# Channel cosines and sines folded into the Fourier weights, h folded over positions ahead of the product

## The chip, the cores and the metric

The kernel runs on one core of one Trainium2 chip. The core has a matrix engine (TensorE, PE in the profile, with its weight loads as PEld), a vector engine (VectorE, DVE), a scalar engine (ScalarE, ACT), a general one (GpSimd, POOL) and a queue engine for transfers (SyncE, SP). The metric is the time of one execution on the device in microseconds, as the median of several runs.

## The reference, cut to what matters

Two sequences (a prompt of 256 and a sample of 1024 positions, each with 16 meta positions ahead of it) go through one encoder layer with shared weights. The change is in branch A and in where the gates are made:

```python
h = rms_norm(x, norm_mix_g)
z = h @ w_in                      # q | k | v | fourier channels | attn gate | fourier gate
f = z[..., o2:o3]                 # 512 channels, 4 groups of 128
...
fg = f.astype(jnp.float32).reshape(b, l, N_FOURIER_GROUPS, FOURIER_GROUP)
y = jnp.real(jnp.fft.fftn(fg, axes=(1, 3), norm='ortho'))   # over positions and channels of a group
...
merged = g_attn * a + g_four * fo
```

The real part of the two-dimensional transform is cos(position) cos(channel) minus sin(position) sin(channel). Cosines are even and sines odd in the position, so a sequence of L positions can be folded first: position n plus position L - n for the cosine part, minus for the sine part. That leaves 521 positions of 1040 for the sample and 137 of 272 for the prompt. In the same way 65 cosines and 63 or 64 sines are enough for a group of 128 channels.

## The kernel before, in words

The kernel multiplies in split form. A float32 operand is stored as a high part, rounded to the format fp32r, and a low part, the rest; `three` (L220) adds high x high, high x low and low x high into one bank of PSUM. So each product of 128 input rows costs three matmuls. A "unit" of weights is 128 output columns for all eight blocks k of 128 input rows: 24 matmuls for one range of positions.

**Stage A** (`stage_a`, L307) normalises x, transposes it (`transpose_pair`, L279) and keeps the result h as `hT[c]`, high and low parts, for three chunks c: 512 and 512 positions of the sample, and the prompt's 256 with the 16 meta positions. As soon as a part of h is there, `fgemm` (L359) multiplies it with four units of Fourier weights: chunk 0 in two halves of 256 positions, the prompt's chunk with 272, chunk 1 with 512. The results go to SBUF as `fT` and `fTp`.

**The next stage** runs three generators, each of which yields a cost after every piece of work. `fourier` (L492) folds f over positions on DVE (`fold`, L499), multiplies it with the channels' cosines and sines (`chan`, L522, in plain float32, tile by tile of 128 positions), and then with the tables of the positions (from L590), which come by the POOL queue. `q_pass` (L753) and `kv_pass` (L694) make q, k and v. `weave(main, side, share)` (L142) puts gate work between their pieces: each cost that main yields, times the share, is spent on steps of `gate_gen` (L432). That generator makes the 16 units of gate logits for one set of chunks and stores them in DRAM; a step is three matmuls. In this stage it works on chunk 0. `ahead` starts the next generator's loads at a given yield of the present one (`QSTART`, L48, is that of q).

**Attention** (L794) writes out its own order of instructions for TensorE, ScalarE and VectorE. Between its steps a `Filler` (L155) places gate steps for chunks 1 and 2, as many as the costs in `FILL` (L430) allow. After it come the merge with the gates, the output projection and the feed-forward part, whose instructions the change doesn't touch.

Outside the parts whose order is written out, a planner places each instruction in its engine's queue: the earliest in program order goes first among those that it expects to be ready. So a load or a matmul of later work may stand ahead of earlier work that is expected to wait. Each engine then takes its queue strictly in order.

SBUF is handed out by `Slots` (L66): 27 single slots and 7 triples, each slot 1056 float32 columns wide. A slot that is given back goes to the end of a queue; who gets it next waits until the last reader is done. The high and low parts of h take 8, 8 and 6 slots for the three chunks.

## Time and profile before

| | |
|---|---|
| Median of 3 runs | 1727.22 us (1727.02 to 1728.23) |
| The profiled execution | 1727.39 us, its span 1725.6 us |
| Granted TensorE clock | 0.996 of full |
| Busy: PE, DVE, ACT, POOL | 97%, 65%, 42%, 16% of the span |
| Instructions | 25871, of them 9837 matmuls |
| HBM traffic | 140.68 MB read, 55.42 MB written |

The span runs from the first to the last instruction; the time of the execution holds a little more at both ends. A row of a group names line, engine, operation, what is written from what, the shapes and the count, then busy time and the mean duration of one. Matmuls overlap, so a mean duration is more than the distance between two of them. A float32 matmul that isn't split is recorded as two. Idle time of an engine is put down to the instruction that ended it.

### The profile page before, as it was taken

The page shows a single profiled execution, that of the slowest core. Times are in us where ns is not written, and L with a number is a line of the kernel's source. Part 1 is how long each engine was busy: PE and PEld are TensorE (multiplying, and loading weights), DVE is VectorE, ACT ScalarE, POOL GpSimd, SP SyncE. Part 2 cuts the span into 40 slices and gives each one's busy share as a digit, 9 for nine tenths or more (in the row PEclk, how much of TensorE's full clock was granted, in tenths as well). Part 3 has the DMA queues.
Part 4 walks back from the last instruction along what each step waited for, and adds up shares of the span by engine and source line. Part 5 has one row for each costly group of instructions (what it writes and reads, how often), then busy time and mean ns, then how long its engine had stood idle before and what let it go on. Part 6 is the DMA issues. An engine that isn't in the chain of part 4 may idle for free.

```text
span 1725.6 us, 25871 instructions
## 1 busy us (share of the span) xinstructions
PE 1679.1 (97%) x9837; PEld 1495.5 (87%) x9837; DVE 1116.3 (65%) x2089; ACT 719.4 (42%) x1429; POOL 278.7 (16%) x321
## 2 busy tenths in 40 slices
PE   7999999999999999989989999999999999999997
PEld 6888879878888888878879999999999998888886
DVE  5423544568888885652479676667666768765685
ACT  6322333456666665451355222222222234444444
POOL 3001333210130212663353000000000000000002
PEclk9999999999999999999999999999999999999999
DMA  5144331312112235534442222322232237653534
GB/s 191 57 140 145 116 116 51 124 53 71 50 57 63 65 116 195 177 110 135 160 158 82 84 71 91 103 91 83 95 103 80 76 123 259 204 179 99 161 99 153
DMA packets 90509, 197.80 MB, mean 115 GB/s; under 512 B 9773, under 2 KB 40137, under 8 KB 90384
## 3 DMA queue, kind: packets, MB, share of 16 engines
q1 hardware_dynamic: 81168, 178.97, 31.5%
q10 hardware_dynamic: 7824, 12.53, 2.1%
q0 software_dynamic: 1392, 4.63, 0.9%
q8 instruction: 77, 1.26, 0.3%
q14 instruction: 48, 0.39, 0.1%
HBM read 140.68 MB, written 55.42 MB: 114 GB/s over the span
## 4 chain that ended last, share of the span: by engine, by line
PE 83%; DVE 7%; issue 3%; ACT 3%; POOL 3%; DMA 2%; SPq 0%; POOLq 0%; ACTq 0%; DVEq 0%
PE i L225 10%; PE i L226 10%; PE i L227 10%; PE o L227 5%; PE o L226 5%; PE o L225 5%; PE g L225 4%; PE S L892 4%; PE g L227 4%; PE g L226 4%; PE pt L826 3%; PE pv L846 2%; PE pv L847 2%; PE wo L226 2%; PE wo L227 2%
## 5 line engine op out<-in xcount | busy, mean ns | idle before, releaser
L1345 ACT CAST w<-wi 128x512 fp32r<-128x512 f32 x168 | 103.9, 621 | 272.0 <-PE i L227 221.1
L225 PE MATMUL i<-A,w 128*128 128x384 f32 x616 | 208.9, 339 | 3.0 <-ACT w L1345 2.7
L227 PE MATMUL i<-A,w 128*128 128x384 f32 x616 | 208.0, 338 | 2.3 <-POOL w L1347 2.3
L226 PE MATMUL i<-A,w 128*128 128x384 f32 x616 | 208.2, 338 | 0.0
L227 PE MATMUL i<-Ah,w 128*128 128x256 f32 x616 | 173.0, 281 | 0.0
L226 PE MATMUL i<-Al,w 128*128 128x256 f32 x616 | 173.0, 281 | 0.0
L225 PE MATMUL i<-Ah,w 128*128 128x256 f32 x616 | 172.7, 280 | 0.0
L828 ACT CAST pT<-pt 128x512 fp32r<-128x512 f32 x156 | 90.7, 582 | 96.4 <-PE pt L826 91.4
L829 DVE TENSOR_TENSOR pT<-pt,pT 128x512 fp32r<-128x512 f32 x156 | 106.9, 686 | 27.1 <-ACT pT L828 25.0
L1347 DVE TENSOR_TENSOR w<-wi,w 128x512 fp32r<-128x512 f32 x154 | 105.2, 685 | 29.0 <-ACT w L1345 28.6
L234 POOL TENSOR_SCALAR fin0r<-fin0ss 128x1 f32<-128x1 f32 x1 | 0.8, 788 | 754.0 <-ACT X L242 754.0
L225 PEld LDWEIGHTS i<-A,w 128*128 128x128 f32 x616 | 116.5, 189 | 3.6 <-ACT w L1345 2.9
L897 DVE TENSOR_REDUCE sm<-S 128x1 f32<-128x1040 f32 (+1 forms) x80 | 86.5, 1081 | 51.1 <-PE S L892 46.8
L227 PEld LDWEIGHTS i<-A,w 128*128 128x128 f32 x616 | 116.2, 189 | 3.2 <-POOL w L1347 3.2
L226 PEld LDWEIGHTS i<-A,w 128*128 128x128 f32 x616 | 116.5, 189 | 0.0
L225 PEld LDWEIGHTS i<-Ah,w 128*128 128x128 f32 x616 | 116.0, 188 | 0.4 <-ACT w L1345 0.4
L227 PEld LDWEIGHTS i<-Ah,w 128*128 128x128 f32 x616 | 116.1, 189 | 0.0
L226 PEld LDWEIGHTS i<-Al,w 128*128 128x128 f32 x616 | 116.0, 188 | 0.0
L904 ACT ACTIVATE p<-S,sm 128x1040 f32<-128x1040 f32 (+1 forms) x80 | 80.2, 1002 | 33.6 <-DVE sm L897 29.2
L826 PE MATMUL pt<-ident,p 128*128 128x128 f32 (+1 forms) x624 | 93.4, 272 | 0.0
L227 PE MATMUL o<-wfo,act 128*128 128x512 f32 (+1 forms) x212 | 82.0, 387 | 2.3 <-DVE act L1479 2.3
L826 PEld LDWEIGHTS pt<-ident,p 128*128 128x128 f32 (+1 forms) x624 | 72.4, 134 | 10.7 <-DVE pT L829 0.2
(762 smaller groups left out, 4444.9 us busy)
## 6 DMA issues: line engine op xcount, KB each, us to landing
wi<-w_fi SPq DMA_DIRECT2D x48, 512.0 KB, 3.4
wg<-w_g SPq DMA_DIRECT2D x32, 512.0 KB, 3.7
act_d<-sc SPq DMA_DIRECT2D x77, 192.0 KB, 1.9
act<-act_d SPq DMA_DIRECT2D x37, 320.0 KB, 3.3
wfo<-w_fo SPq DMA_DIRECT2D x21, 512.0 KB, 5.2
X<-act_d SPq DMA_DIRECT2D x31, 320.0 KB, 3.0
act_d<-sc SPq DMA_DIRECT2D x77, 128.0 KB, 1.7
gate<-gs ACTq DMA_DIRECT2D x32, 256.0 KB, 2.0
```

Source lines behind the costliest of these rows:

```text
L225: mm(out, sh, mh, start=first and i == 0, stop=False)
L226: mm(out, sh, ml, start=False, stop=False)
L227: mm(out, slo, mh, start=False, stop=last and i == n - 1)
L826: nc.tensor.transpose(pt[:rows, h * P : (h + 1) * P], me.ps4[h][:, col : col + rows], self.ident[:])
L828: nc.scalar.copy(pT[:rows, :512], pt[:rows, :])
L829: nc.vector.tensor_tensor(pT[:rows, 512:1024], pt[:rows, :], f32(pT[:rows, :512]), op=ALU.subtract)
L846: nc.tensor.matmul(me.pv[:], vst, pT[:rows, :512], start=j == 0, stop=False)
L892: nc.tensor.matmul(S[:, base + lo : base + hi], hq, self.kT[seq][g][v][:, lo:hi], start=v == 0, stop=v == 1)
L897: nc.vector.tensor_reduce(nb, S[:, base : base + L], axis=AX.X, op=ALU.max, negate=True)
L904: self.last_exp = nc.scalar.activation(p, S[:, base : base + L], AF.Exp, bias=nb, accum_out=total)
L1345: nc.scalar.copy(w[:, :512], src)
L1347: eng.tensor_tensor(w[:, 512:1024], src, f32(w[:, :512]), op=ALU.subtract)
```

## The change

The channels' cosines and sines are multiplied into the Fourier weights on the chip. `channels` does this with 32 float32 matmuls on the transposed weights `w_ft`, and splits the result into high and low parts `wc`: for each k 260 cosine columns (4 groups of 65) and 252 sine columns (4 of 63).

Before the product, h itself is folded over positions. For each k, `folds` copies the meta positions on ACT, adds the high and low parts of h on POOL, makes sum and difference on DVE, and splits both (`eo`) on ACT and DVE. Two folds are issued between the units of the last product of stage A, the others between the products that use them.

`fourier_in` multiplies the folded h with the new weights: six blocks of positions (four of 128, one of 41, one of 128), for each the even part with 260 columns and the odd part with 252, three matmuls each, accumulated over all eight k in six banks of PSUM. The result, evicted in high and low parts, takes the place of what `chan` made. The tables of positions are rearranged to fit, with the weight of the two ends halved, and the rows of the output weights likewise.

In stage A, `first` takes the place of `fgemm`, with the same ranges of positions (256 in place of 272 for the prompt): it makes the first four units of gate logits and stores them. `gate_gen` makes the other twelve. The numbers that pace the gate work (`FILL`, the shares of `weave`, `QSTART`) are changed with it.

```diff
-QSTART = 22
+QSTART = 60
...
+N_FIRST = 4
...
+NS, NP_ = 521, 137
+FN = 544 + NP_
...
-            if len(wf) < 4:
-                wf.append(self.load_split(a["w_f"][len(wf)], D, "wf", nc.vector))
+            if len(wf) < N_FIRST:
+                wf.append(self.load_split(a["w_g"][len(wf)], D, "wf", nc.vector))
...
-        self.fT = [sl.get(f"fT{g}") for g in range(4)]
-        self.fTp = [sl.get(f"fTp{g}") for g in range(2)]
...
-        def fgemm(c, lo, hi):
+        def first(c, lo, hi, then=None):
...
-            for g in range(4):
-                wh, wl = wf[g]
-                pf = ps.tile([P, 512], F32, tag="mm", name=f"f{c}_{g}")
+            for u in range(N_FIRST):
+                wh, wl = wf[u]
+                pf = ps.tile([P, 512], F32, tag="mm", name=f"f{c}_{u}")
...
-                if c < 2:
-                    b = N_META + 512 * c + lo
-                    nc.scalar.copy(self.fT[g][:, b : b + n], pf[:, :n])
...
-                    fp = self.fTp[g // 2]
-                    nc.scalar.copy(fp[:, b + N_META : b + 272], pf[:, :256])
-                    nc.vector.tensor_copy(fp[:, b : b + N_META], pf[:, 256:272])
-                    nc.vector.tensor_copy(self.fT[g][:, :N_META], pf[:, 256:272])
+                st = self.small.tile([P, 512], F32, tag="stage", name=f"fg{u}_{c}")
+                nc.scalar.copy(st[:, :n], pf[:, :n])
+                nc.scalar.dma_start(self.gates[u][c][:, lo:hi], st[:, :n])
+                if then is not None:
+                    sl.put(wh, wl)
+                    if u % 2 == 0:
+                        next(then)
...
-        fgemm(0, 0, 256)
...
-        fgemm(0, 256, 512)
...
-        fgemm(2, 0, 272)
+        self.T = self.const.tile([P, P], F32, name="T")
+        nc.sync.dma_start(self.T[:], a["chan"])
+        wt = [sl.get("wft") for _ in range(4)]
+        for g in range(4):
+            nc.sync.dma_start(wt[g][:, :D], a["w_ft"][g])
+        first(2, 0, 256)
         tiles(4)
-        fgemm(1, 0, 512)
...
-    FILL = {"s": 610, "p": 400, "end": 640, "drain": 900}
+        self.channels(ps, wt)
+        sl.put(*wt)
+        self.fold = self.folds()
+        next(self.fold)
+        first(1, 0, 512, self.fold)
...
+    def channels(self, ps, wt):
...
+        self.wc = [(sl.get("wch", F32R, "s"), sl.get("wcl", F32R, "s")) for _ in range(4)]
+        for k in range(KD):
+            pt = ps.tile([P, 512], F32, tag="mm", name=f"wc{k}")
+            for g in range(4):
+                c = slice(g * P, (g + 1) * P)
+                nc.tensor.matmul(pt[:, c], wt[g][:, k * P : (k + 1) * P], self.T[:], start=True, stop=True)
+            p4 = pt[:].rearrange("p (g c) -> p g c", g=4)
+            for src, b, w in ((p4[:, :, :65], 0, 65), (p4[:, :, 65:], 260, 63)):
+                h, l = (x.v(4, w, k % 2 * 512 + b) for x in self.wc[k // 2])
+                nc.scalar.copy(h, src)
+                nc.vector.tensor_tensor(l, src, f32(h), op=ALU.subtract)
+        self.wz = self.small.tile([P, 512], F32R, tag="stage", name="wz")
+        nc.gpsimd.memset(f32(self.wz[:, 260:]), 0.0)
+        nc.gpsimd.tensor_copy(self.wz[:, :260], f32(self.wc[0][0][:, :260]))
...
+    def folds(self):
...
+        vec, pool = nc.vector.tensor_tensor, nc.gpsimd.tensor_tensor
+        hs = [sl.get("hs", F32, "s") for _ in range(2)]
+        ep, od = sl.get("ep", F32, "s"), sl.get("od", F32, "s")
...
+        for i, (h, l) in enumerate(zip(t["hi"], t["lo"])):
+            per = t["per"]
...
+            pool(out, *src, op=ALU.add)
...
+        for k in range(KD):
+            s, p = hs[k % 2], ep[:, 8 : 8 + LP + 1]
+            m = m32[:, k * N_META : (k + 1) * N_META]
+            for x, L in ((s, LS), (p, LP)):
+                nc.scalar.copy(x[:, :N_META], m)
+                nc.scalar.copy(x[:, L : L + 1], m[:, 0:1])
+            for c, x, lo in ((0, s, N_META), (1, s, N_META + 512), (2, p, N_META)):
+                h, l = (f32(y) for y in self.hpair(self.hT[c], k, 0, CH_N[c]))
+                pool(x[:, lo : lo + CH_N[c]], h, l, op=ALU.add)
+            out = self.eo[k] = []
+            for z, op in ((e, ALU.add), (o, ALU.subtract)):
+                vec(z[:, :NS], s[:, :NS], s[:, LS : NS - 2 : -1], op=op)
+                vec(z[:, 544:FN], ep[:, 8 + NP_ - 1 : 7 : -1], p[:, NP_ - 1 :], op=op)
+                h, l = (sl.get("eo", F32R, "s") for _ in range(2))
+                nc.scalar.copy(h[:, :FN], z)
+                vec(l[:, :FN], z, f32(h[:, :FN]), op=ALU.subtract)
+                out.append((h, l))
+            yield
...
+    def fourier_in(self, ps):
...
+        cols = [(j * P, P) for j in range(4)] + [(512, 41), (553, P)]
+        banks = [ps.tile([P, 512], F32, tag="mm" if j < 4 else "tr", name=f"u{j}") for j in range(6)]
+        for k in range(KD):
+            while k not in self.eo:
+                next(self.fold)
+            parts = self.eo.pop(k)
+            w = [x[:, k % 2 * 512 : k % 2 * 512 + 512] for x in self.wc[k // 2]]
+            for j, (b, m) in enumerate(cols):
+                for odd, (h, l) in enumerate(parts):
+                    s = slice(260, 512) if odd else slice(260)
+                    out, hm, lm = banks[j][:m, s], h[:, b : b + m], l[:, b : b + m]
+                    if k or odd:
+                        nc.tensor.matmul(out, hm, w[0][:, s], start=False, stop=False)
+                    else:
+                        nc.tensor.matmul(banks[j][:m, :], hm, self.wz[:], start=True, stop=False)
+                    nc.tensor.matmul(out, hm, w[1][:, s], start=False, stop=False)
+                    nc.tensor.matmul(out, lm, w[0][:, s], start=False, stop=odd == 1 and k == KD - 1)
+                yield 0
+            for x in parts:
+                sl.put(*x)
+            if k + 2 < KD:
+                next(self.fold)
+            if k % 2:
+                sl.put(*self.wc[k // 2])
+        next(self.fold, None)
+        ue = [sl.get("ue", F32R) for _ in range(3)]
+        uo = [sl.get("uo", F32R) for _ in range(3)]
...
+        for j, (_, m) in enumerate(cols):
...
+            for base, w, src in ((0, 64, ev[:, :, :64]), (256, 1, ev[:, :, 64:65])):
+                hv = u.v(4, w, b + base)[:m]
+                lv = u.v(4, w, b + 260 + base)[:m]
+                nc.scalar.copy(hv, src)
+                nc.vector.tensor_tensor(lv, src, f32(hv), op=ALU.subtract)
+            b = j % 2 * 512
+            u = uo[j // 2]
+            src = banks[j][:m, 260:512]
+            nc.scalar.copy(u[:m, b : b + 252], src)
+            nc.vector.tensor_tensor(u[:m, b + 256 : b + 508], src, f32(u[:m, b : b + 252]), op=ALU.subtract)
+        self.U = ue, uo
+        yield 6000
...
+    FILL = {"s": 455, "p": 350, "end": 480, "drain": 900}
...
-        order = list(range(16))
+        order = list(range(N_FIRST, 16))
...
-        E = [sl.get(f"fe{j}") for j in range(2)]
-        O = [sl.get(f"fo{j}") for j in range(2)]
-        Ep, Op = sl.get("fep"), sl.get("fop")
...
-        def fold(src, b, L, e, eb, o, ob, eng):
...
-            eng.tensor_tensor(
-                e[:, eb + 1 : eb + h], src[:, b + 1 : b + h], src[:, b + L - 1 : b + h : -1], op=ALU.add
-            )
-            eng.tensor_tensor(
-                o[:, ob + 1 : ob + h], src[:, b + 1 : b + h], src[:, b + L - 1 : b + h : -1], op=ALU.subtract
-            )
...
-        for g in range(4):
-            b = (g % 2) * 521
-            fold(self.fT[g], 0, LS, E[g // 2], b, O[g // 2], b, nc.vector)
-            fold(self.fTp[g // 2], (g % 2) * 272, LP, Ep, g * 137, Op, g * 137, nc.vector)
-            yield 1
-        sl.put(*self.fT, *self.fTp)
...
-        def chan(seq):
...
-            for j in range(nt):
...
-                        e, o = Ep[:, b : b + m], Op[:, b : b + m]
-                    nc.tensor.matmul(pe[:m, g * 65 : (g + 1) * 65], e, T[:, :65], start=True, stop=True)
-                    nc.tensor.matmul(po[:m, g * 64 : (g + 1) * 64], o, T[:, 65:129], start=True, stop=True)
...
-                yield 2000
...
-        for j, m in enumerate((P, 9)):
+        for j, m in enumerate((P, 41)):
             nc.gpsimd.dma_start(tp[j][:m, : 4 * NLP], a["pos_p"][j, :m])
-        us = yield from chan("s")
-        up = yield from chan("p")
-        sl.put(*E, *O, Ep, Op)
+        yield from self.fourier_in(ps)
+        us = self.U
...
-        ms = [P, 9]
+        ms = [P, 41]
...
-                    (u_of(kind, p, up, j, m), (tp[j][:m, tb : tb + NLP], tp[j][:m, tb + NLP : tb + 2 * NLP]))
+                    (u_of(kind, p, us, 5 - j, m), (tp[j][:m, tb : tb + NLP], tp[j][:m, tb + NLP : tb + 2 * NLP]))
...
-        sl.put(*tp, *up[0], *up[1])
+        sl.put(*tp)
...
             weave(ahead(self.fourier(ps), QSTART, q_pass), gates, 0.6)
-            weave(ahead(q_pass, KVSTART, kv_pass), gates, 0.62)
-            weave(kv_pass, gates, 0.6)
+            weave(ahead(q_pass, KVSTART, kv_pass), gates, 0.35)
+            weave(kv_pass, gates, 0.7)
...
-    t["chan"] = np.concatenate([np.cos(ang) * r, np.sin(ang[:, :64]) * r], axis=1).astype(np.float32)
...
+    t["chan"] = np.concatenate([np.cos(ang) * r, np.sin(ang[:, 1:64]) * r], axis=1).astype(np.float32)
...
         ang = 2 * np.pi * ((n * ls[None]) % L) / L
-        keep = (n <= L // 2) * (L ** -0.5)
+        keep = ((n >= 0) & (n <= L // 2)) * (L ** -0.5) * np.where(n % (L // 2) == 0, 0.5, 1.0)
...
-    cp, sp = pos(LP, 2, np.arange(1, NLP + 1))
+    i = np.arange(P)
+    n = np.concatenate([127 - i, np.where((i >= 32) & (i <= 40), 168 - i, -1)])
+    cp, sp = pos(LP, n, np.arange(1, NLP + 1))
...
-        "w_f": units(w[:, 768:1280]),
+        "w_ft": w[:, 768:1280].T.reshape(4, P, D),
```

More of the change, by code (lines that the diff above doesn't have):

```diff
@@ L414, in stage_a @@
         nc.sync.dma_start(xm[:N_META, :D], a["meta_tokens"])
-        fgemm(0, 0, 256)
+        first(0, 0, 256)
         tiles(2)
@@ new lines, in folds @@
+    def folds(self):
+        nc, sl = self.nc, self.sl
+        vec, pool = nc.vector.tensor_tensor, nc.gpsimd.tensor_tensor
+        hs = [sl.get("hs", F32, "s") for _ in range(2)]
+        ep, od = sl.get("ep", F32, "s"), sl.get("od", F32, "s")
+        m32 = self.const.tile([P, KD * N_META], F32, name="m32")
+        t = self.hT[2]
+        for i, (h, l) in enumerate(zip(t["hi"], t["lo"])):
+            per = t["per"]
+            n = min(per, KD - per * i)
+            src = [f32(x.v(per, t["n"])[:, :n, 256:272]) for x in (h, l)]
+            out = m32[:, i * per * N_META : (i * per + n) * N_META].rearrange("p (k c) -> p k c", k=n)
+            pool(out, *src, op=ALU.add)
+        e, o = ep[:, 304 : 304 + FN], od[:, :FN]
+        for x in (e, o):
+            nc.gpsimd.memset(x[:, NS : 512 + 32], 0.0)
+        self.eo = {}
+        yield
[16 more added lines that the diff above has]
+                out.append((h, l))
+            yield
+        sl.put(*hs, ep, od)
```

62 lines of the change are left out of this document (16 added, 46 removed).

## The prediction

> **What bounds the kernel now.** I read the page's table of engines first, then the stretches by engine, then what TensorE waited for, and last the order of single instructions around the change.
>
> ```profile
> span 1725.6 us, 25871 instructions
> PE 1679.1 (97%) x9837; PEld 1495.5 (87%) x9837; DVE 1116.3 (65%) x2089; ACT 719.4 (42%) x1429; POOL 278.7 (16%) x321
> ```
>
> ```profile
> 60.00:100.00 40.00, 39.04 (x218) 32.49 (x217) 16.14 (x40) 12.85 (x34) 4.56 (x8) 1.00 0.16 39
> 100.00:150.00 50.00, 50.00 (x302) 40.50 (x302) 14.71 (x29) 12.54 (x25) 3.72 (x7) 1.00 0.62 206
> 150.00:260.00 110.00, 108.68 (x531) 89.11 (x530) 51.13 (x91) 32.81 (x58) 36.92 (x43) 1.00 0.29 104
> 360.00:650.00 290.00, 287.33 (x1729) 241.41 (x1728) 235.78 (x348) 185.36 (x335) 46.98 (x40) 1.00 0.23 69
> ```
>
> A stretch's columns are its length, then the busy time of PE, PEld, DVE, ACT and POOL, the granted clock, and the DMA share and rate. From 60 to 650 us TensorE is busy nearly all the time at clock 1.00; it waits for almost nothing in the stages that the change rewrites:
>
> ```profile
> PE qtr L778 <- DVE qs L769: 1.3, 1, 1.3
> PE g L225 <- ACT fT L373: 1.0, 1, 1.0
> ```
>
> These are all its waits between 60 and 260 us. So the time falls by what is taken off TensorE, as long as the vector engines keep up, and rises by each new wait. VectorE is idle over half of the time up to 260 us, but has 235.8 of 290 us in attention.
>
> **The price of a matmul.** Matmuls overlap, so I take the distance between starts, not a mean duration.
>
> ```profile
> 39.62 0.28 PE L227 MATMUL f<-hT0h,wfl 128*128 128x256 f32 x1
> ...
> 44.34 0.28 PE L225 MATMUL f<-hT0h,wfh 128*128 128x256 f32 x1
> ```
>
> ```profile
> 77.63 0.39 PE L225 MATMUL f<-hT1h,wfh 128*128 128x512 f32 x1
> ...
> 82.97 0.39 PE L227 MATMUL f<-hT1h,wfl 128*128 128x512 f32 x1
> ```
>
> The first pair is 40 steps apart: 4.72/40 = 0.118 us for 256 columns. The second is 23 steps: 5.34/23 = 0.232 us for 512.
>
> **TensorE, part by part.** One unit over one range of positions is 8 k times 3 products = 24 matmuls, so four units are 96.
>
> - Removed, the Fourier product of L359: two ranges of 256 (192 x 0.118 = 22.7 us), one of 272 (96 x 0.125, scaled, = 12.0), one of 512 (96 x 0.232 = 22.3): 57.0 us.
> - Added in its place, four gate units over three ranges of 256 and one of 512: 34.0 + 22.3 = 56.3 us.
> - Removed from the later gate work, the same four units, two ranges of 512 and one of 256: 44.5 + 11.3 = 55.8 us. Of this 22.3 us were woven into the Fourier, q and k/v stages, and 33.6 us are attention's filler.
> - Added, the folded product: 8 k x 6 position blocks x 6 matmuls = 288, of 260 or 252 columns, six of them 512: 282 x 0.118 + 6 x 0.232 = 34.7 us.
>
> ```profile
> 85.14 0.33 PE L538 MATMUL ues<-T,fe 128*128 128x65 f32 x2
> ...
> 86.64 0.39 PE L539 MATMUL uos<-T,fo 128*128 128x64 f32 x2
> 86.84 0.48 PE L225 MATMUL g<-hT0h,wgh 128*128 128x512 f32 x1
> ```
>
> ```profile
> 97.23 0.28 PE L538 MATMUL ues<-T,fe 128*9 128x65 f32 x2
> ...
> 98.03 0.28 PE L539 MATMUL uos<-T,fo 128*9 128x64 f32 x2
> ```
>
> ```profile
> 59.05 1.47 PE L287 MATMUL x4tr<-ident,h 128*128 128x128 f32 x12
> ```
>
> - Removed, the channel product of L522: a tile of eight float32 matmuls takes 86.84 - 85.14 = 1.70 us, five such tiles 8.5 us, and the two tiles of nine rows 0.9 us each: 10.3 us.
> - Added, channels: 32 float32 matmuls of 128 columns, not in this trace. By the channel rows (16 records in 1.70 us, two per matmul) they take 6.8 us; were the time in proportion to columns, 13.6. The transposes have 128 columns and the same 0.11 us a record (1.47 us for 12), so I take 7.0.
>
> The sum on TensorE is -57.0 + 56.3 - 55.8 + 34.7 - 10.3 + 7.0 = **-25.1 us**. The position products keep their number: a block of 41 rows instead of 9 is as many matmuls.
>
> **The fold on the vector engines.** For each k, folds adds h's two halves on POOL (512, 512 and 256 columns), makes sum and difference on DVE (521 and 137 columns each), and splits both results of 681 columns: a cast on ACT, a subtraction on DVE.
>
> ```profile
> L690 POOL TENSOR_TENSOR ropeA<-ropeA 128x512 f32<-128x512 f32 x10 | 12.9, 1286 | 0.0
> L1139 POOL TENSOR_TENSOR gt<-gt 128x256 f32<-128x256 f32 x8 | 6.2, 775 | 1.0 <-DMA norm_ffn_g<-norm_ffn_g 1.0
> L501 DVE TENSOR_TENSOR fe<-fT 128x519 f32<-128x519 f32 x4 | 2.8, 699 | 10.4 <-ACT fT L373 10.4
> L501 DVE TENSOR_TENSOR fep<-fTp 128x135 f32<-128x135 f32 x4 | 1.2, 300 | 0.0
> L210 DVE TENSOR_TENSOR wql<-wq,wqh 128x1024 fp32r<-128x1024 f32 x3 | 3.5, 1221 | 2.0 <-ACT wqh L209 2.0
> L209 ACT CAST wqh<-wq 128x1024 fp32r<-128x1024 f32 x3 | 3.1, 1049 | 3.3 <-DMA wq<-w_q 3.3
> L450 ACT CAST wgh<-wg 128x512 fp32r<-128x512 f32 x40 | 23.4, 618 | 29.5 <-DMA wg<-w_g 21.3 <-PE f L226 4.8 <-DVE qs L769 1.5
> ```
>
> POOL: 1.29 + 1.29 + 0.77 = 3.35 us. DVE: 2 x (0.70 + 0.30) + 2 x 0.87 (between 0.70 for 519 and 1.22 for 1024) = 3.74 us. ACT: two casts of 0.76 and four small copies of some 0.16 = 2.2 us. TensorE uses up one k in 34.7/8 = 4.34 us. Side by side the fold needs 3.74 us a k and is hidden; with none of it overlapped 3.35 + 3.74 + 2.2 = 9.3 us. Between them stands what POOL and DVE do to each other:
>
> ```profile
> 10.17 2.37 POOL L210 TENSOR_TENSOR wfl<-wf,wfh 128x1024 fp32r<-128x1024 f32 x1 [0.99 <-ACT wfh L209]
> 11.56 2.06 DVE L210 TENSOR_TENSOR wfl<-wf,hT0l 128x1024 fp32r<-128x1024 f32 x1 [1.60 <-ACT hT0l L209]
> ```
>
> DVE's subtraction of 1024 columns, elsewhere 1.22 us, began while POOL's ran and took 2.06: POOL was done at 12.54, 0.98 us after DVE's start, and 2.06 - 0.98 = 1.08 is about DVE's own time. It stood still meanwhile. I therefore take POOL and DVE one after the other, ACT beside them: 7.1 us a k.
>
> The Trainium skill (SBUF — State Buffer, Who interferes with whom) says of this that a VectorE instruction with two SBUF inputs and a GpSimd instruction that reads SBUF exclude each other for a whole instruction, whichever began first. This speaks against the change, since every add of the fold is such an instruction; by the rule all of POOL's 3.35 us stand beside DVE's 3.74, and without it the stall worked out next would be nought. The one pair quoted agrees with it.
>
> **What lies ahead of the fold.** It can start when the last columns of h are there:
>
> ```profile
> 63.19 0.88 DVE L303 SCALAR_TENSOR_TENSOR hT1l<-x4tr,gcol,hT1h 128x256 fp32r<-128x256 f32 x2 [0.18 <-ACT hT1h L301]
> ```
>
> From about 63 us TensorE has channels (7.0) and the last gate range (22.3), so the folded product starts near 92 us: 29 us of cover, which hold three or four folds of 7.1. But SBUF holds only about three k of folded h (48 slots, of which h takes 22, the new weights 8, the fold's own buffers 4, two the tables: 12 left at four per k), so the fourth must wait for the first k's products, 4.3 us in. From there come its tail (some 2.5 us) and four folds, and the last is wanted after 7 k = 30.4 us: stall = 4.3 + 2.5 + 4t - 30.4 = 4t - 23.6 us. For t = 7.1 that is **4.8 us**, for 3.74 none, for 9.3 13.6. I take 5.
>
> **The seam behind it.** Before, TensorE evicted each channel tile behind gate matmuls. Now the gate weaving stands at cost 0 through the whole product, and the first position product reads the two banks that are evicted last.
>
> ```profile
> L546 ACT CAST ue<-ues 128x256 fp32r<-128x256 f32 x4 | 1.5, 373 | 7.8 <-PE ues L538 7.8
> L547 DVE TENSOR_TENSOR ue<-ues,ue 128x256 fp32r<-128x256 f32 x4 | 1.7, 425 | 7.3 <-ACT ue L546 7.3
> tabc<-pos_c POOLq DMA_DIRECT2D x4, 520.0 KB, 4.9
> ```
>
> Six banks of two casts of 0.37 and a small one are some 5.4 us on ACT; banks finish 0.7 us apart, so the last cast ends about 2 us behind TensorE and its subtraction 0.4 later. The cost of 6000 that follows releases 3600 of gate work, about 3.9 us of matmuls, if their weights are split by then; ACT has the casts in front of them. Nothing to 5 us: I take 3. The position tables are on POOL's queue behind the folds, and their slots come free only as k 6 and 7 are consumed; five of 520 KB, 4.9 us each to land, overlapping, against some 8 us until they are read: nothing to 5, I take 1. The weight loads for channels stand on SP's queue ahead of the gates' loads, but in a stage with DMA share 0.16. The q weights are asked for four steps ahead of the stage's end, as before (60 of 64 yields against 22 of 26). I cost both at nothing; uncovered, each is one landing, 5 us.
>
> **Attention.** Its filler falls from 610 to 455 a step, two steps a head: 310 of cost, at 0.696 us per 640 (three matmuls) 0.34 us less a head.
>
> ```profile
> 404.05 1.24 DVE L897 TENSOR_REDUCE sm<-S 128x1 f32<-128x1040 f32 x1 [0.46 <-PE S L892]
> 405.33 1.13 ACT L904 ACTIVATE p<-S,sm 128x1040 f32<-128x1040 f32 x1 [0.25 <-DVE sm L897]
> 406.82 0.54 PEld L892 LDWEIGHTS S<-kT,qT 128*128 128x128 f32 x3
> ```
>
> The next head's scores use the same bank and may start when the exponential ends, 405.33 + 1.13 = 406.46; they start at 406.82. This spare 0.36 us just covers 0.34. DVE would be busy 235.8 of some 256 us. At worst the whole 33.6 us stay as idle time, at best nothing is lost; by the spare time I take 3 us (64 heads at 0.05).
>
> **The sum**: -25.1 + 5 + 3 + 1 + 3 = -13.1 us. The profiled execution took 1727.39 us, 1.8 beyond its span and 0.2 above the median of 1727.22: 1727.4 - 13.1 = 1714.3, so **1714 us**.
>
> **Rivals.**
> 1. Full gain: the planner fills every stall with gate matmuls, as it does at 86.84. Against it: those gates have lost a quarter of their supply and come late. 1727.4 - 25.1 = 1702 us.
> 2. Attention gives half of its filler back, 17 us instead of 3: DVE at 92% has no room for a late cast. For it the spare of 0.02 us; against it, that TensorE waits there hardly at all now. 1714.3 + 14 = 1728 us.
> 3. The folds don't run ahead (slower). If fold k + 2 gets its slots only from k's products, as the order of the program has it, each costs t in place of 4.34 us for six k: 6(t - 4.34). With t = 9.3, one chain, it is 29.8 in place of 5: 1714.3 + 24.8 = 1739 us. With 7.1 it is 16.6: 1726. It turns the change into a loss from t of about 7.4 on, where 6(t - 4.34) reaches 25.1 - 7. For it: two fold buffers, one pair for sums; against it, the 29 us of cover and free slots.
> 4. The fewer matmuls don't come into the time at all, because the new product is paced by its weight loads, not its columns: then 288 would cost as many slots as before. Against it: 0.118 us already holds a load for each matmul. At twice 0.118 the product is 69 us: 1714.3 + 34.5 = 1749 us.
>
> **Chances.** Forecast 0.44 (1708 to 1722), full gain 0.20, attention 0.13, folds behind 0.18, the fourth 0.02, the rest anything else. A measurement here tells 0.2% (3.5 us) from nothing. Faster: the first two, a fifth of the attention case and 0.03 of the rest, 0.70; same, from 1723.8 to 1730.7, 0.12 from rivals 2 and 3; slower 0.18. The range runs from 1701 to 1733, which leaves out the far ends of rivals 1 and 3 and the fourth.
>
> **What would show it.** Right: between 60 and 130 us TensorE's waits name eo (the folded parts) for 3 to 8 us in all, late in the product; DVE's adds of 521 columns take over 0.7 us where POOL runs; attention is some 30 us shorter with waits of S for the exponential below 6 us. Wrong: no wait on eo (then 1 or less), over 15 us of it (rival 3), attention's idle time over 10 us (rival 2), or starts of the new matmuls further apart than 0.12 us.

## The result, and the profile after

| | before | changed |
|---|---|---|
| Median, beside each other on one chip | 1727.02 us (1723.82 to 1728.23, 5 runs) | 1735.84 us (1732.87 to 1737.35, 5 runs) |
| Profiled execution, its span | 1727.39, 1725.6 us | 1737.35, 1735.6 us |
| Mean granted clock | 0.996 | 0.988 |

The ratio is 1.0050, with a 95% interval of 1.0035 to 1.0065: the changed kernel is slower by 8.8 us, where 13 us less were forecast. The page of the changed kernel:

```profile
PE 1672.8 (96%) x9789; PEld 1489.0 (86%) x9789; DVE 1137.2 (66%) x2086; ACT 723.0 (42%) x1462; POOL 299.7 (17%) x347
...
PEclk9997999999999999999999999999999999999999
```

TensorE is busy for 1672.8 us after 1679.1, only 6.3 less where the forecast took 25.1 us of work off it. The row of granted clocks has a 7 in the fourth slice (130 to 174 us), where the kernel before has only nines: part of the busy time is work at a slow clock.

To see where the time went I compare the starts of three kinds of matmul: the first scores (attention begins), the first fo (attention's work is done) and the last o. First the changed kernel's order of single instructions on PE (start, duration, engine, line, operation), then the one before:

```profile
340.00 0.46 PE L949 MATMUL S<-kTp,qT 128*128 128x272 f32 x1
...
680.79 0.31 PE L1118 MATMUL fo<-pT 68*128 68x328 f32 x1
...
1728.61 0.28 PE L231 MATMUL o<-wfo,wfo 128*128 128x256 f32 x1
```

```profile
314.40 0.52 PE L892 MATMUL S<-kTp,qT 128*128 128x272 f32 x2 [0.24 <-ACT gs L457]
...
674.96 0.32 PE L1061 MATMUL fo<-pT 68*128 68x328 f32 x1
...
1718.65 0.28 PE L227 MATMUL o<-wfo,wfo 128*128 128x256 f32 x1
```

| Stretch | before | changed | difference | forecast |
|---|---|---|---|---|
| up to the first S | 314.4 | 340.0 | +25.6 | +8.5 work, +9 losses = +17.5 |
| first S to first fo | 360.6 | 340.8 | -19.8 | -33.6 work, +3 loss = -30.6 |
| first fo to last o | 1043.7 | 1047.8 | +4.1 | 0 |

The columns add up to +10, which is the difference of the spans, and to the forecast's -13.1. So 8 us were lost in the stages ahead of attention beyond what was forecast, 11 in attention, 4 behind it.

**The fold** cost TensorE nothing. These are all of PE's waits from 60 to 130 us in the changed kernel (engine and line, whose result it waited for, us in all, times, longest):

```profile
PE wc L450 <- DVE wcl L455: 1.3, 1, 1.3
PE u L517 <- ACT fg L375: 1.2, 1, 1.2
PE f L229 <- DVE wcl L455: 0.2, 1, 0.2
```

None names eo. **The seam** behind it has one wait, of 4.5 us, and what comes after it is worse. The rows are stretches with length, busy time of PE, PEld, DVE, ACT and POOL, granted clock, DMA share and rate:

```profile
131.96:135.37 3.41, 0.00 (x0) 0.00 (x0) 1.97 (x7) 1.86 (x8) 0.00 (x0) 1.00 1.05 364
135.37:155.82 20.45, 19.38 (x66) 15.84 (x67) 4.26 (x12) 3.65 (x9) 0.00 (x0) 0.50 0.19 55
155.82:160.00 4.18, 4.18 (x29) 3.64 (x28) 0.00 (x0) 0.38 (x1) 0.00 (x0) 1.00 0.17 64
336.76:340.17 3.41, 0.74 (x5) 0.61 (x6) 1.95 (x10) 1.13 (x5) 1.33 (x3) 1.00 0.94 342
340.17:343.58 3.41, 3.41 (x11) 2.74 (x10) 0.93 (x3) 1.11 (x4) 0.00 (x0) 0.50 0.47 189
```

TensorE stands still from 131.8 to 136.3 us, and from 135.37 on its clock is at half for 20.45 us, though PE is shown as busy for 19.38 of them. The same happens on a small scale at the end of the k/v passes, where it idles 2.7 us and then works 3.41 us at half clock. The evictions that it waits for, on ACT, and the matmul that waits, on PE:

```profile
131.88 0.16 ACT L539 CAST ue<-u 128x4 fp32r<-128x4 f32 x1 [0.54 <-DVE ue L540]
132.27 0.37 ACT L544 CAST uo<-u 128x252 fp32r<-128x252 f32 x1 [0.23 <-DVE ue L540]
...
133.46 0.16 ACT L539 CAST ue<-u 128x4 fp32r<-128x4 f32 x1 [0.54 <-DVE ue L540]
```

```profile
136.29 0.48 PE L229 MATMUL fpe<-hT0l,ue 128*128 128x136 f32 x1 [4.46 <-ACT ue L539]
```

Every second and third cast of a bank waits for DVE's subtraction of the piece before it in the same bank. So a bank takes 133.46 - 131.88 = 1.58 us, not the 0.9 that its three casts take, and the banks that the first position product needs come last.

**Attention**: its stretch and its waits in the changed kernel.

```profile
340.00:681.00 341.00, 327.50 (x1932) 269.22 (x1930) 265.70 (x424) 210.13 (x398) 46.88 (x40) 0.99 0.24 73
```

```profile
PE S L949 <- ACT p L961: 6.2, 10, 1.5
PE pv L903 <- DVE ao L911: 5.2, 9, 0.9
```

TensorE is not at work for 13.5 us here. The waits for the exponential (p) and for the eviction of pv (ao) are 11.4 us; before, the same two were 3.3 and 1.1 us.

### The profile page after: what moved, and what is told of

It is laid out like the page before. It is cut to its first block, busy times and chain, and to the rows that moved or that the text cites. A ratio compares the mean times of both kernels' runs of the same rounds, so it can differ in the third digit from the quotient of the medians.

```text
span 1735.6 us, 25870 instructions
## 1 busy us (share of the span) xinstructions
PE 1672.8 (96%) x9789; PEld 1489.0 (86%) x9789; DVE 1137.2 (66%) x2086; ACT 723.0 (42%) x1462; POOL 299.7 (17%) x347
## 4 chain that ended last, share of the span: by engine, by line
PE 60%; DVE 6%; issue 3%; ACT 3%; POOL 2%; DMA 1%; POOLq 0%; ACTq 0%; SPq 0%; DVEq 0%
PE i L231 10%; PE i L229 10%; PE i L230 10%; PE o L231 5%; PE o L230 5%; PE o L229 4%; PE S L949 3%; PE pt L883 2%; PE wo L230 1%; PE pv L903 1%; PE wo L231 1%; PE wo L229 1%; PE pv L904 1%; PE g L229 1%; POOL gt L1196 1%
## 5 line engine op out<-in xcount | busy, mean ns | idle before, releaser
L886 DVE TENSOR_TENSOR pT<-pt,pT 128x512 fp32r<-128x512 f32 x156 | 106.9, 686 | 26.9 <-ACT pT L885 25.1
L231 PE MATMUL o<-wfo,act 128*128 128x512 f32 (+1 forms) x212 | 82.2, 388 | 1.6 <-DVE act L1536 1.6
L230 PE MATMUL o<-wfo,act 128*128 128x512 f32 (+1 forms) x212 | 82.1, 387 | 0.2 <-DVE wfo L1540 0.2
```

Source lines behind the costliest of these rows:

```text
L230: mm(out, sh, ml, start=False, stop=False)
L231: mm(out, slo, mh, start=False, stop=last and i == n - 1)
L886: nc.vector.tensor_tensor(pT[:rows, 512:1024], pt[:rows, :], f32(pT[:rows, :512]), op=ALU.subtract)
```

## The experiments

Times are medians; each ratio is to the kernel before on the same chip, in brackets its 95% interval.

**1. Evictions by bank.** The cut edit, in the function of the folded product and its evictions:

```
-            for j, (b, m) in enumerate(cols):
+            for j in (5, 4, 0, 1, 2, 3):        # product and evictions
...
-                nc.scalar.copy(hv, src)
-                nc.vector.tensor_tensor(lv, src, f32(hv), op=ALU.subtract)
+                todo.append((hv, lv, src))      # uo's piece too
+            for hv, lv, src in todo: nc.scalar.copy(hv, src)
+            for hv, lv, src in todo: nc.vector.tensor_tensor(lv, src, f32(hv), op=ALU.subtract)
```

> The changed kernel with one thing altered: the six banks of the folded product are finished and evicted in the order 5, 4, 0, 1, 2, 3, and in each bank the three casts of ACT come before the three subtractions of DVE, so that no cast waits for a subtraction of its own bank. Nothing is left out. Theory A (the seam costs twice: TensorE idles 4.5 us for the evictions, and because of that idle stretch the granted clock then stands at 0.50 for some 20 us, about 10 us of lost work): TensorE's idle stretch ahead of fpe falls below 2 us, the clock stays at 1.00 from 128 to 160 us, and the time falls by 4.5 + 10 = 14 us, to about 1722 us. Rival B (the low clock there has another cause, such as the small matmuls of fpe themselves): the idle goes, the clock still falls to 0.50, and the time falls by 4 to 5 us, to about 1731 us. Rival C (it is not on the path): 1736 us, no change.

Measured: 1723.46 us, 0.9978 (0.9969 to 0.9987). Two stretches of this kernel, and its first S:

```profile
128.00:136.00 8.00, 8.00 (x46) 6.45 (x44) 6.08 (x23) 3.78 (x17) 2.64 (x5) 1.00 1.02 346
136.00:156.00 20.00, 20.00 (x125) 15.75 (x124) 3.27 (x8) 3.58 (x7) 0.00 (x0) 1.00 0.41 131
```

```profile
326.76 0.50 PE L951 MATMUL S<-kTp,qT 128*128 128x272 f32 x1
```

No idle time, clock 1.00, and 125 matmuls in 20 us; the changed kernel made 66 in its 20.45 us at half clock. The first S, in the last row, comes at 326.8 us in place of 340.0, so the seam cost 13.2 us. Theory A holds. The edit holds two things (the order of the banks, with their places in PSUM, and the order within a bank), which I did not tell apart.

**2. Work in the seam that nobody needs**, so that the wait stays and only the idleness goes.

```
+        pad = ps.tile([P, 512], F32, tag="g", name="pad")
+        for _ in range(22):
+            nc.tensor.matmul(pad[:], hi[:, :P], hi[:, :512], start=True, stop=True)  # hi: first 512 columns of hT[0]
         for j, (_, m) in enumerate(cols):     # evictions
```

> The changed kernel with 22 matmuls of 512 columns added behind the folded product, about 5.1 us (22 x 0.232), whose results nobody uses; the evictions are as they were. TensorE then waits as long for the evictions, but is at work meanwhile. Theory A (the idle stretch itself makes the clock fall): the clock stays at 1.00 up to 160 us and the time falls by about 10 us, to about 1726 us, though work was added. Rival B (the low clock comes from what runs after the seam): the clock still falls to 0.50, and the time stays at 1736 us or rises by up to 5 us.

Measured: 1729.33 us, 1.0015 (1.0006 to 1.0024), 6.5 us below the changed kernel with 5.1 us of work added. Its stretch of the position products:

```profile
140.00:156.00 16.00, 16.00 (x100) 13.49 (x99) 3.15 (x8) 2.10 (x4) 0.00 (x0) 1.00 0.26 84
```

The same position products run behind the same evictions at full clock, so rival B falls: it is the idleness ahead of them that halves the clock. Theory A's size was somewhat off. fpe begins at 137.2 us (136.3 in the changed kernel) and S at 333.0, which is 195.8 us later in place of 203.7. The slow clock thus costs 7.9 us; of the rest of the 13.2, 4.5 are the idle time itself and 0.8 stay open.

**3. Gates in the seam.** The step behind the product asks for 14000 in place of 6000 of gate work, and q's share falls.

```
-        yield 6000
+        yield 14000
...
-            weave(ahead(q_pass, KVSTART, kv_pass), gates, 0.35)
+            weave(ahead(q_pass, KVSTART, kv_pass), gates, 0.25)
```

> The changed kernel with two numbers altered: the step that lies between the folded product and the position products asks for 14000 instead of 6000 of gate matmuls, and the q passes take gate work at a share of 0.25 instead of 0.35, so that what the seam uses more is there for the k/v passes' end too. Nothing is left out. Theory A: TensorE has gate matmuls while the evictions run, the idle stretch and the fall of the clock both go (14 us), and so do the waits for ks at 340 us and the clock's second dip (3 to 5 us): 1717 to 1722 us. Rival B (the clock falls anyway): 1728 to 1732 us. Rival C (the gates that are used early are missed later, in the q passes): less than 5 us, 1731 to 1736 us.

Measured: 1720.23 us, 0.9961 (0.9948 to 0.9973), theory A. fpe begins at 137.3 us, later than in the changed kernel, and it doesn't matter: TensorE has work and keeps its clock, and S begins at 325.1 us. Two numbers of the planner bring 15.6 us.

**4. The kernel before with a quarter less filler**: the gates of units 12 to 15 are left out for the chunks that attention fills with (those of units 0 to 3 are stored in their place), and the filler's prices are the changed kernel's.

```
-    FILL = {"s": 610, "p": 400, "end": 640, "drain": 900}
+    FILL = {"s": 455, "p": 350, "end": 480, "drain": 900}
...
-        order = list(range(16))
+        order = list(range(16 if chunks == [0] else 12))
...
+            if c and u < 4:
+                nc.scalar.dma_start(self.gates[u + 12][c][:], st[:, :n])
```

> The kernel before, with a quarter of the attention's filler taken out and nothing else: the gate logits of units 12 to 15 are not computed for the second and third chunks (the values of units 0 to 3 are stored in their place), and the filler's prices are those of the changed kernel (455, 350, 480). So 33.6 us of TensorE work leave the attention stage, as in the changed kernel, and everything ahead of it is as before. Theory A (the heads run into their own chain, maxima to exponentials to the next product, and into the evictions at the end of every fourth head): the stage gets shorter by 18 to 22 us only, and the kernel takes about 1707 us. Rival B (attention was slowed in the changed kernel by what came before it, or by the clock): the whole 33 us come, about 1694 us. Rival C (it is no shorter at all, since the chain bound the stage before as well): above 1720 us.

Measured: 1707.28 us, 0.9888 (0.9874 to 0.9901), 19.8 us less than before for 33.6 us of work. First S to first fo takes 338.9 us (312.9 to 651.8), 21.7 less than before, as in the changed kernel (19.8). Its stretch and waits:

```profile
312.90:651.80 338.90, 325.35 (x1929) 267.85 (x1929) 265.42 (x423) 210.06 (x397) 46.85 (x40) 1.00 0.26 80
```

```profile
PE S L894 <- ACT p L906: 6.7, 13, 1.5
PE pv L848 <- DVE ao L856: 5.2, 9, 0.8
```

So 11.9 of the 33.6 us are lost with nothing of the fold or the seam ahead: that much of the changed kernel's 13.8 comes from the thinner filler alone. The other 1.9 fit the slow clock from 340.17 to 343.58 us, which lies in this stretch of the changed kernel: experiment 9, without it, takes 338.6 us. Theory A.

**5. The exponential ahead of the second cast.** The ACT rows of one group's change in the changed kernel show where the heads lose:

```profile
434.08 1.13 ACT L961 ACTIVATE p<-S,sm 128x1040 f32<-128x1040 f32 x1
...
437.05 0.59 ACT L885 CAST pT<-pt 128x512 fp32r<-128x512 f32 x1 [1.29 <-PE pt L883]
437.95 0.58 ACT L885 CAST pT<-pt 128x512 fp32r<-128x512 f32 x1 [0.32 <-PE pt L883]
438.61 0.58 ACT L910 COPY ao<-pv 64x512 f32<-64x512 f32 x1
439.22 1.13 ACT L961 ACTIVATE p<-S,sm 128x1040 f32<-128x1040 f32 x1
...
443.31 1.13 ACT L961 ACTIVATE p<-S,sm 128x1040 f32<-128x1040 f32 x1 [0.25 <-DVE sm L954]
447.12 1.13 ACT L961 ACTIVATE p<-S,sm 128x1040 f32<-128x1040 f32 x1 [0.25 <-DVE sm L954]
```

From one exponential to the next it is 3.8 to 4.1 us, but 5.1 where a group of four heads begins its second half: there two casts and the ao copy stand ahead of it in ACT's queue, and the next scores wait for it, since there is one score tile. The edit gives only one key block to the half ahead of the exponential:

```
-                for _ in range(-(-me.left() // (2 * (ready + 4 - n) - k))):
+                x = 2 * (ready + 4 - n) - k
+                for _ in range(-(-me.left() // x) if k else me.left() // x):
                     me.turn()
```

> The changed kernel with the gates in the seam (14000 and 0.25, as in the run before) and one thing more: where a new group of four heads begins its second half of attention, only one of its transposed key blocks is cast ahead of the head's exponential on ACT, and the second one, with the eviction of the group before, comes behind it. All the work is still done. Theory A (attention gives back filler because in every fourth head two casts and the ao copy stand in front of the exponential in ACT's queue, and the single score tile waits for that exponential): the fourth heads shorten from 4.6 to 5.8 us towards 4.0, the waits of S for exp and of pv for ao fall from 11 to below 4 us, and the time falls by 6 to 12 us against the kernel with the gates in the seam, to 1708 to 1714 us. Rival B (the evictions themselves or the one pv tile set the period wherever they stand): no gain, about 1720 us. Rival C (what is put behind the exponential makes TensorE wait for pT in that half instead): 1720 to 1730 us.

Measured, on top of experiment 3: 1745.70 us, 1.0107 (1.0091 to 1.0122) and 25.5 us slower than without it, worse than every theory. Its waits in attention and two stretches:

```profile
PE pv L903 <- DVE ao L911: 20.8, 17, 1.9
```

```profile
421.00:424.40 3.40, 2.28 (x13) 1.44 (x12) 3.06 (x6) 3.30 (x6) 0.00 (x0) 1.00 0.00 0
424.40:427.83 3.43, 3.43 (x14) 3.04 (x13) 1.34 (x2) 0.33 (x1) 1.28 (x1) 0.50 0.20 38
```

Moved behind the exponential, ao is late for the new group's first product, which needs the only pv tile and stands ahead of the next scores in PE's queue. So TensorE waits 17 times, up to 1.9 us, and after some of these waits works at half clock for 3.4 us as well. The mechanism (the place in ACT's queue) was not refuted by this, but my cure made a new wait.

**6. A shorter idle stretch**: as experiment 2, with 6 added matmuls for 22.

> The changed kernel with 6 idle-time matmuls of 512 columns behind the folded product, in place of the 22 of the run before: some 1.4 us of the 4.5 us idle stretch are filled, 3.1 us stay. Nothing is left out. Theory A (the clock falls once TensorE has been idle for about 3.5 us, as the 2 us windows of the changed kernel show it): the clock stays at 1.00, and the time is that with 22 matmuls, about 1729 us. Rival B (it falls after a shorter stretch, as the 2.7 us at 340 us suggest, where it went to 0.57): the clock falls again and the time is 1731 to 1737 us, by how long it stays down.

Measured: 1736.70 us, 1.0053 (1.0038 to 1.0068). Rival B: with 3.1 us of idle time the clock falls as it did with 4.5, and stays down as long.

```profile
132.00:135.40 3.40, 0.64 (x3) 0.19 (x1) 2.07 (x7) 2.08 (x9) 0.00 (x0) 1.00 0.85 301
135.40:155.85 20.45, 20.00 (x69) 16.45 (x70) 4.00 (x12) 3.01 (x7) 0.00 (x0) 0.50 0.19 53
```

**7. Dense work behind the idle stretch**: 22 matmuls of 512 columns that read the last evicted piece of U, between the step behind the product and the position products.

```
         yield 6000
+        pad = ps.tile([P, 512], F32, tag="g", name="pad")
+        for _ in range(22):
+            nc.tensor.matmul(pad[:], hi[:, :P], ue[2][:, 520:1032], start=True, stop=True)
```

> The changed kernel with 22 matmuls of 512 columns (5.1 us of work at full clock), whose results nobody uses, behind the idle stretch of the seam: they need the last evicted piece of U, so TensorE idles as long as before, and then has dense work instead of the short position products. Nothing is left out. Theory A (a few us of dense work bring the clock back): the clock is at 1.00 again about 4 us after the idle ends, at 140 to 142 us, and the time stays about 1736 us, or falls by up to 4 us, since what the added matmuls cost (5 to 7 us) is won again in the position products. Rival B (the clock stays down for some 20 us whatever runs): the added matmuls take 9.5 us at half clock, all the rest is as late as before, and the time is 1741 to 1746 us.

Measured: 1736.70 us, 1.0054 (1.0037 to 1.0070), theory A:

```profile
134.30:137.06 2.76, 0.01 (x1) 0.01 (x1) 2.17 (x7) 1.89 (x6) 0.00 (x0) 0.50 0.28 100
137.06:141.10 4.04, 4.04 (x10) 3.17 (x11) 0.84 (x3) 0.37 (x1) 0.00 (x0) 0.50 0.00 0
141.10:146.00 4.90, 4.90 (x26) 4.02 (x24) 0.30 (x1) 0.00 (x0) 0.00 (x0) 1.00 0.00 0
```

The clock is back 4.0 us after work begins, where it took 19.5 us (136.3 to 155.8) with the position products. What the dense matmuls cost they win back, no more.

**8. Evictions by bank and a share of 0.28 for the q passes**, with the attention order of experiment 5.

> The changed kernel with the evictions by bank (order 5, 4, 0, 1, 2, 3, casts before subtractions), the q passes' share of gates at 0.28 instead of 0.35, and the second key block of a new group behind the exponential. All the work is done. Theory A: the seam and the attention's fourth heads are both mended, and the k/v passes' end has gates left: 1706 to 1713 us, as with the gates in the seam or some 2 us less. Rival B (the attention part brings nothing): about 1719 us.

Measured: 1747.81 us, 1.0119 (1.0101 to 1.0137). The same wait as in 5 (of pv for ao, 20.9 us) spoils it.

**9. Evictions by bank and a share of 0.28**, attention as it was.

> The changed kernel with the evictions by bank (as in the first of these runs) and the q passes' share of gates at 0.28 instead of 0.35; the attention is left as it was. Theory: the wait of ktr for ks at the end of the k/v passes (2.7 us, with some 2 us of low clock behind it) goes, since gates are left to fill it, and S begins at about 322.7 us; the time is 2 to 4 us below that of the evictions by bank alone, 1719 to 1721 us. Rival (the share only moves gates from one place where they are wanted to another): 1722 to 1724 us.

Measured: 1720.88 us, 0.9969 (0.9957 to 0.9980), 2.6 us below experiment 1. The wait for ks at the end of the k/v passes is gone:

```profile
322.83 0.37 PE L951 MATMUL S<-kTp,qT 128*128 128x272 f32 x1
```

S begins 3.9 us earlier than in experiment 1, and only 8.4 us later than before the change.

**10 and 11. The order in attention, two more ways**, both on top of 9 and both with the edit of 5, one key block ahead of the exponential. In 10 the last product of the old group and its ao are made ahead of the exponential, in the place of the second cast. In 11 ao stays behind it, and the new group's first product waits a turn:

```
+                if k == 0 and me.j == 1 and late[0][0] is not me:     # 10, behind the turns of a half
+                    product()
...
-                if len(late) == 2:                                     # 11, in turn()
+                while len(late) > (2 if me.j == 2 and len(me.keys) == 9 else 1):
                     product()
```

> The kernel with evictions by bank and share 0.28, and in attention: at the head where a new group's second half begins, one key block is cast ahead of the exponential instead of two, and the last product of the group before and its ao eviction are made right behind it, ahead of the exponential too; the second block comes behind it. So ACT has one cast less (0.58 us) ahead of the exponential, and no product waits for ao just ahead of S, as it did when ao stood behind the exponential (20.8 us of waits, and the clock fell after 1.1 to 1.9 us of idle). Theory A: the fourth heads get 0.5 to 0.7 us shorter, 17 of them, and the time falls by 6 to 10 us against share 0.28 alone, to 1710 to 1714 us. Rival B (the exponential then waits for the later product and its copy, which end no sooner than the two casts did): within 3 us of share 0.28 alone. Rival C (it starves TensorE): slower than that.

> The kernel with evictions by bank and share 0.28, and in attention: one key block ahead of the exponential, as above; ao is evicted behind the exponential, and the first product of the new group, which needs the only pv tile, comes a turn later, in the next head, so that ao has some 2 us to be done. Theory A (the ACT queue ahead of the exponential sets the fourth heads, and the wait for ao spoilt the earlier try): the fourth heads come to about 4 us like the others, the waits of pv for ao go, and the time falls by 8 to 12 us against share 0.28 alone, to 1708 to 1712 us. Rival B: TensorE has too little ready in the head in between (one product less there), idles for more than a us and loses clock again; 1720 us or more.

Measured: 1712.18 us, 0.9918 (0.9904 to 0.9931), and 1709.38 us, 0.9898 (0.9883 to 0.9913). Theory A for both: 8.7 and 11.5 us below experiment 9, 17.4 us below the kernel before and 26.5 below the changed one. ACT's exponentials and attention's stretch in 11:

```profile
426.96 1.13 ACT L964 ACTIVATE p<-S,sm 128x1040 f32<-128x1040 f32 x1 [0.26 <-DVE sm L957]
...
431.03 1.13 ACT L964 ACTIVATE p<-S,sm 128x1040 f32<-128x1040 f32 x1 [0.25 <-DVE sm L957]
...
435.85 1.13 ACT L964 ACTIVATE p<-S,sm 128x1040 f32<-128x1040 f32 x1 [0.85 <-DVE sm L957]
```

```profile
322.30:652.80 330.50, 321.87 (x1931) 267.31 (x1929) 263.81 (x424) 210.60 (x397) 46.05 (x39) 1.00 0.25 76
```

Where the new group begins, the exponential follows the one before by 4.07 us; the casts that were moved make the next one late (4.82), and by then the row names DVE's maximum, not ACT's queue. The stage takes 330.5 us, against 338.6 in 9, and 30.1 less than before: nearly the 33.6 us of work.

**12. A control**: the order of 11 in the kernel before.

> The kernel before, with the same order in attention as the last run (one key block ahead of the exponential where a new group begins, ao evicted behind it, the new group's first product a turn later) and nothing else. It is a control: how much of the 11.5 us that this order brought would be had without the change? Theory A (it heals what the thinner filler uncovered; before, TensorE had 277.3 of 280 us at work between 360 and 640 us, so there is little to win): 0 to 3 us faster than the kernel before, 1724 to 1727 us. Rival B (the order is better whatever the filler): 8 to 11 us faster, 1716 to 1719 us. Rival C: slower.

Measured: 1725.99 us, 0.9994 (0.9985 to 1.0003), so 1.1 us, and by the interval 2.6 at most. The 11.5 us of this order are not to be had without the change: with the full filler TensorE was busy for 354.8 of attention's 360.6 us before, and had little to win. With the same order in both, the change is worth 1725.99 - 1709.38 = 16.6 us once the seam and the shares are mended (11).

## Why the prediction was wrong, step by step

**What bounds the kernel, the price of a matmul, the sum on TensorE: right.** With the seam and the k/v tail mended (9), S begins 8.4 us later than before; the terms ahead of attention summed to 33.6 - 25.1 = +8.5. In 11 attention's stretch is 30.1 us shorter than before, and 27.9 shorter than with the same order and the full filler (358.4 us in 12). The folded product ran from 92.7 to 127.5 us (34.7 forecast, from 92); rival 4, pacing by weight loads, fell. So did rival 1, the full gain.

**The fold: mechanism right, effect none.** I took a stall of 5 us with t = 7.1 us a k. DVE and POOL do hold each other up:

```profile
73.33 0.69 DVE L491 TENSOR_TENSOR od<-hs 128x521 f32<-128x521 f32 x1
...
76.72 1.76 POOL L488 TENSOR_TENSOR hs<-hT1h,hT1h 128x512 f32<-128x512 f32 x1
77.24 1.97 DVE L495 TENSOR_TENSOR eo<-od,eo 128x681 fp32r<-128x681 f32 x1
...
79.33 0.69 DVE L491 TENSOR_TENSOR od<-hs 128x521 f32<-128x521 f32 x1
...
119.58 0.87 DVE L495 TENSOR_TENSOR eo<-od,eo 128x681 fp32r<-128x681 f32 x1 [0.88 <-ACT eo L494]
```

The subtraction of 681 columns takes 0.87 us alone (forecast 0.87) and 1.97 where it begins within POOL's add; the rule of the Trainium skill that I cited (SBUF — State Buffer, Who interferes with whom) is borne out again. But one k took 79.33 - 73.33 = 6.0 us and not 7.1: I had added up durations, and one engine's operations start closer together than these say (the next one 0.61 us behind the od row of 0.69 us). That explains a part of the 1.1 us; the rest I did not work out. With t = 6.0 the formula 4t - 23.6 gives 0.4 us. The last fold was done at 120.45, and its first product was made at 123.2. Rival 3 fell with the same rows.

**The seam: this step failed.** I had "nothing to 5, I take 3" and it cost 13.2. Three things were missing. I added up the casts of ACT alone, 0.9 us a bank, and took the last to end 2 us behind TensorE; but the program writes cast, subtraction, cast on one bank, and each waits for the other engine, 1.58 us a bank and, with some gate casts between, 10.7 us in all (127.5 to 138.2). I also let the evictions start as the banks finish. The last matmul of the first bank ended at 124.1 us, but ahead of its cast in ACT's queue stood casts of gate weights, two of which waited 1.65 us for their load:

```profile
126.41 1.14 ACT L571 CAST wgh<-wg 128x512 fp32r<-128x512 f32 x2 [1.65 <-DMA wg<-w_g]
127.46 0.36 ACT L539 CAST ue<-u 128x256 fp32r<-128x256 f32 x1
```

So the first cast came 3.3 us late. What each of these two adds to the idle 4.5 us was not measured; in experiment 1 the evictions began as late (127.11), and its order of them was enough. And I priced an idle stretch at its own length. Experiments 1 and 2 show that the 4.5 us brought 7.9 us of slow clock behind them. The trace of the kernel before shows it, in a stretch behind waits for w_out's weights, and I passed over it:

```profile
772.00:776.00 4.00, 1.08 (x4) 0.69 (x5) 0.68 (x2) 2.06 (x4) 3.34 (x2) 1.00 0.90 353
776.00:780.00 4.00, 4.00 (x12) 3.17 (x11) 3.77 (x3) 2.09 (x2) 2.88 (x2) 0.57 0.73 221
```

The Trainium skill has the rule (TensorE: Matmul & The Clock Gate, Part 1: The HAM clock gate: half clock after an idle window of about 3.4 us, full clock again after one busy window), and weighed against the seam's upper end of 5 us it would have been a rival. The tables' 1 us didn't come: fpe's is the only wait of TensorE between 127 and 170 us.

**The k/v passes' end: not costed.** Gates taken early were missing there: a wait of 2.7 us with slow clock behind it. By experiment 9 it is 3.9 us ahead of S, of which 2.6 came into the time. I had followed the gates' quarter of lost supply in attention, and not to the last place where the weaving needed them.

**Attention: mis-sized**, 3 us forecast and 13.8 lost (33.6 - 19.8), 11.9 of them by the thinner filler (experiment 4). I took one head's spare time of 0.36 us, between an exponential and the next scores, for all 64 heads. The starts of these heads' exponentials in the traces show that most had less to spare. Mean us from one exponential to the next, in groups of four heads:

| | before | changed | 12 | 11 |
|---|---|---|---|---|
| up to the head where a group's second half begins | 5.37 | 5.15 | 4.01 | 3.88 |
| to the next head | 4.47 | 4.25 | 5.26 | 4.87 |
| to the third | 4.05 | 4.00 | 4.39 | 3.99 |
| to the fourth | 4.05 | 3.93 | 4.08 | 3.91 |
| all 63 together | 283.0 | 273.4 | 279.7 | 262.6 |

No distance in the kernel before or in the changed one is under 3.80 us, and the third and fourth stood little above it. In a head of 3.81 us (443.31 to 447.12 above) the next scores start at 444.70, 0.26 us behind the exponential's end, their maximum runs from 445.85 to 447.09, and the next exponential follows at 447.12: the chain through the one score tile fills the whole period. Of the 4 x 0.34 = 1.36 us of filler that a group gave up, only 0.61 came into the time. About two thirds of the loss lie in the third and fourth heads, the rest in the two heads where a group begins, where the casts and ao in ACT's queue hold the exponential. With the order of 11 a group gives back 1.09 us (12 against 11). Rival 2 (17 us, 1728) was near in size, but its cause, DVE's load, is not what the runs show: DVE was busy for 78% of the stretch, and in 11 nearly the same DVE work (263.8 us for 265.7) fits into 330.5 us. That the place of two casts and ao in ACT's queue decides how much of the filler's time is won is shown by experiments 10, 11 and 12.

**Behind attention: +4.1 us, open.** One more stretch of 3.41 us at half clock near 780 us can hold up to 1.7 of them, and TensorE's idle time there hardly differs (19.5 us after 19.2). From first fo to last o took 1043.5 and 1043.7 us in the profiles of the two kernels with full filler (12 and before) and 1045 to 1051 in those with less, experiment 4 among them. What late work the shorter attention leaves there was not tested.

**What would show it**: I had said that no wait on eo would mean 1 us or less for the fold, and over 10 us of idle time in attention rival 2. Both came (0 and 13.5 us). With the fold at 0 and attention at 13.8 the sum would be -25.1 + 3 + 1 + 13.8 = -7.3 us, 1720 us, still faster; it was the seam, for which I had named no sign, that turned the result, with the k/v passes' end and the stretch behind attention to add to it. The terms that the runs give in place of mine, -25.1 + 13.2 + 3.9 + 13.8 + 4.1, come to +9.9 us, for the +10.0 of the spans.

## What to carry to other kernels

An idle stretch of TensorE costs more than its length when it is long enough for the clock to fall, so look for the seams between stages, price each by the slowest chain of evictions in it, and keep a few us of independent matmuls for it, or order evictions so that the first-needed bank comes first and no engine waits for another within a bank. When work that fills waits is taken out of a stage, go through every place that lived on it, every kind of head for itself, since the gain ends at the first chain that is now longer than the work.

## What the runs showed of the hardware

- The slow clock comes in units. It lasted 3.4 us (340.17 to 343.58), 6.8 (experiment 7, 134.3 to 141.1) and 20.45 us (the seam), which are one, two and six times 3.41; and its starts at 135.37 and 340.17 lie 204.8 us apart, 60 times 3.41. A third stretch, from 780.49 to 787.31 us, begins 129 such units behind the second. The clock is thus set anew on a grid of 3.41 us, which agrees with the free-running window that the Trainium skill describes in the section named above.
- The Trainium skill speaks of an idle window there. Here a window needn't be idle throughout: the clock fell after one with 0.74 of 3.41 us of work (at 340 us), and in experiment 5 after one with 2.28 of 3.40, where the gap was 1.1 us.
- Getting back depends on what runs, and not on the time alone. The position products, shown as busy 19.38 of 20.45 us, didn't lift the clock for six windows; dense matmuls of 512 columns did within 4.0 us. The same products held a full clock where it had not fallen before (experiment 1).
